# The first MLP's blocks 1 to 3 by seven products of quarters, and four modulations computed inside the retention heads

## The chip, the cores and the metric

The kernel runs on one core of a Trainium2 chip. The metric is device time in microseconds for one execution. A profile is taken of a separate execution; its own time stands beside its span.

## What is computed

One step of a two-layer network on 512 latent and 128 context tokens, 1024 channels each. Layer 0 mixes tokens by pooling, layer 1 by retention in four heads; each mixer is followed by an MLP of 4096 hidden channels with a squared ReLU. Before each sub-layer stands an RMS norm with a shift and a scale, behind it a gate; these six vectors of a layer (its modulations) come from the conditioning vectors by one linear map.

```python
def trunk(x, cond, ...):
    for i in range(DEPTH):
        mod = (silu(cond) @ w_ada[i] + b_ada[i])[:, None, :]
        sh_a, sc_a, g_a, sh_m, sc_m, g_m = split(mod, 6)
        h = rmsnorm(x, norm_mix_w[i]) * (1 + sc_a) + sh_a
        mix = pool_mixer(h) if i % 2 == 0 else retention_mixer(h)
        x = x + g_a * mix
        h = rmsnorm(x, norm_mlp_w[i]) * (1 + sc_m) + sh_m
        x = x + g_m * (square(relu(h @ mlp_w1[i])) @ mlp_w2[i])
    return rmsnorm(x, final_norm_w)
```

## The kernel before

**Layout.** The residual stream lies with channels on partitions: 8 tiles of 128 channels by 640 tokens (`xall`). Tokens are worked in two halves of 320. Every float32 product is made of three reduced-precision ones: both operands are split into a high and a low part (`split`, L142: ScalarE writes the high part, VectorE subtracts for the low one), and `mm3` (L202) issues high·high, high·low and low·high (L205, L206, L207). `gemm` (L209) runs them over the tiles of the inner dimension; an output tile of 128 channels over 1024 inner channels is 24 matmuls of 320 columns for each half.

**Weights.** `load` (L163) brings 1 MB of a weight matrix from HBM into one of two `wst` buffers by SyncE's DMA queue; `weights` (L183) splits it into two pairs `whi`, `wlo`. A third load waits until the splits of the first one are done.

**MLP.** `mlp` (L738) goes over four blocks of 1024 hidden channels. Each has a first product (`hidden`, L841, squares the ReLU and splits it) and a second one whose 8 output tiles are added to `xall` by `add_to_x` (L471, its instruction at L474). For the blocks named in `FAST` the first product is made by a scheme with seven products of quarters in place of eight: `quarters` (L756) forms sums of quarters of the activations once for the MLP, `seven` (L778) forms and splits seven sums of quarters of the weights for each half block (two loads of 1 MB, its first sum at L789), and `fast` (L800) runs the products and combines their results on VectorE. Before, only the second MLP (layer 1) does so, in blocks 1 to 3.

**Modulations.** `ada` (L272) is a generator; a call of `step` (L376) runs it by a piece. A modulation in mode "s s" is formed on VectorE: `sums` (L307) multiplies rows of 512 weights by one conditioning value and adds them up (L312, L314: 32 instructions of 512 columns), `turn_sums` (L316) turns the result by TensorE transposes (L320, 16 of them) and VectorE reduces (L321). `STEPS` says behind which output tile of the first MLP how many pieces run. Before, all six of layer 1 and the last one of layer 0 are made so inside the first MLP. Their weights land in `both` buffers of the MLP's own pool.

**Heads.** For each of the four retention heads: queries and keys (for heads 1 to 3 made at the end of the head before), state operands and decay tables on VectorE and ScalarE (`states`, L987; `attention`, L1023), the first two gate products (`gates`, L1010), the attention, two more gate products, the values of the next head (`values`, L964), the output product.

**Order.** The program is recorded in the order of the code, and a scheduler then places the instructions of each engine in one queue. An instruction waits on semaphores at its place in that queue.

Of the kernel before, what the change touches and what calls it, by code (L numbers as in the profile page):

```python
# [9 lines left out]
F32 = mybir.dt.float32  # L10
# [4 lines left out]
ALU = mybir.AluOpType  # L15
AX = mybir.AxisListType
PSUM = bass.MemoryType.PSUM

D = 1024
KD = D // 128  # L20
# [13 lines left out]
HALF = TOK // 2  # L34
# [16 lines left out]
MODE5 = "s s"  # L51
# [8 lines left out]
AHEAD = 1  # L60
FREE = 5

FAST = ((), (1, 2, 3))

STEPS = (((0, 0, 0, 0, 3, 2, 3, 0), (2, 1, 2, 1, 2, 1, 1, 1)),
# [3 lines left out]


def constants():
# [39 lines left out]
def hybrid_kernel(ctx: ExitStack, tc: tile.TileContext, x_prompt, x_sample, state_ret, c, c_ctx, w_ada, b_ada,  # L111
# [3 lines left out]
    V, S, G, T = nc.vector, nc.scalar, nc.gpsimd, nc.tensor  # L115
    uid = [0]

    def nm(s):
        uid[0] += 1
        return f"{s}_{uid[0]}"  # L120

    const = ctx.enter_context(tc.tile_pool(name="const", bufs=1))
# [4 lines left out]
    tmp = ctx.enter_context(tc.tile_pool(name="tmp", bufs=1))  # L127
# [3 lines left out]
    def bank():  # L131
        return psum.tile([128, 512], F32, tag="ps", name=nm("ps"))
# [30 lines left out]
    def load(src, shape, st=None):  # L163
        if not st:
            pool, n = extra[0] if extra else (wst, 2)
            if extra:
                extra.append(extra.pop(0))
            st = pool.tile([128, 2048], F32, tag="wst", name=nm("wst"), bufs=n)
        st = st.rearrange("p (a b) -> p a b", a=shape[0])
        nc.sync.dma_start(out=st, in_=src.rearrange("(k p) n -> p k n", p=128))  # L170
        return st
# [57 lines left out]
    ident = tab_sb[:, C_ID:C_ID + 128]  # L229
# [10 lines left out]
    c4 = const.tile([128, KD, 4], F32, name="c4")  # L240
# [7 lines left out]
    vec = const.tile([128, 168], F32, name="vec")  # L248
    O_MIX, O_MLP, O_PB, O_PS, O_FN, O_GN, O_B = 0, 16, 32, 40, 48, 56, 72
# [18 lines left out]
    ready = set()  # L268
# [3 lines left out]
    def ada(works, lag):  # L272
# [99 lines left out]
        if late:  # L372
            turn(*late.pop())

    def stepper(gen):
        def step(n=1, until=None):  # L376
            while n if until is None else until not in ready:
                try:
                    next(gen)
                except StopIteration:  # L380
                    return
                n -= 1
        return step
# [141 lines left out]
    with tc.tile_pool(name="pool", bufs=1) as pp:  # L525
# [9 lines left out]
        for word in FIRST.split():  # L535
            if word[0] == "a":
                astep(int(word[1:]))
            else:
                i = len(xt)
# [98 lines left out]
        run(PLAN[0])  # L638
        astep(until=(0, 2))

        ga = const.tile([128, KD, 2], F32, name="ga0")
        gb = const.tile([128, KD, 2], F32, name="gb0")
        V.tensor_tensor(ga, mod[0][2], vec[:, O_PS:O_PS + KD].unsqueeze(2).to_broadcast([128, KD, 2]), ALU.mult)
        V.tensor_tensor(gb, ga, vec[:, O_PB:O_PB + KD].unsqueeze(2).to_broadcast([128, KD, 2]), ALU.mult)
        V.tensor_scalar(ga, ga, -1.0, None, ALU.mult)
# [92 lines left out]
    def mlp(i, sq, norm, hm, step, along):  # L738

        with tc.tile_pool(name=f"hid{i}", bufs=1) as hid:  # L740
# [8 lines left out]
            def get(b, n):  # L749

                for o in range(1, AHEAD + 1):
                    if b * 8 + n + o < 64 and not ((b * 8 + n + o) // 16 in FAST[i] and (b * 8 + n + o) // 8 % 2 == 0):
                        gets[(b * 8 + n + o) // 8]((n + o) % 8)
                return gets[b](n)
# [45 lines left out]
            def fast(b, half, ops, take):  # L800

                col = b * 1024 + half * 512
                ws = seven(mlp_w1[i, :, col:col + 512])

                banks = {}
                w, u, v = next(ws), {}, {}
                for p, name in enumerate(("p1", "p5", "p6", "p7", "p5", "p1", "p7")):
                    after = next(ws, None)
                    for t in range(2):
                        fresh = (name, t) not in banks  # L810
                        if fresh:
                            banks[name, t] = bank()[:, 0:HALF]
                        ps = banks[name, t]
                        for k in range(4):
                            mm3(ps, [z[:, k, t * 128:t * 128 + 128] for z in w], ops[p][k], fresh and k == 0, k == 3, not fresh)
                        n = half * 4 + t
                        if p == 0:
                            u[t] = th()
                            S.copy(u[t], ps)
                        elif p == 2:  # L820
                            V.tensor_tensor(u[t], u[t], ps, ALU.add)
                        elif p == 3:
                            v[t] = th()
                            V.tensor_tensor(v[t], ps, u[t], ALU.subtract)
                            V.tensor_tensor(v[t], v[t], banks["p5", t], ALU.subtract)
                            take(n + 2, 1, v[t])
                        elif p == 4:
                            f = th()
                            V.tensor_tensor(f, u[t], ps, ALU.add)
                            take(n, 1, f)  # L830
                        elif p == 5:
                            take(n, 0, ps)
                        elif p == 6:
                            V.tensor_tensor(u[t], ps, u[t], ALU.subtract)
                            take(n + 2, 0, u[t])
                    w = after

            for b in range(4):
                act = [[hid.tile([128, TOK], F32R, tag=f"a{n}{e}", name=nm("a")) for e in "hl"] for n in range(8)]

                def hidden(n, h, ps):  # L841
                    r, f = th(), th()
                    S.activation(r, ps, AF.Relu)  # L843
                    S.activation(f, r, AF.Square)  # L844
                    split(f, *[z[:, HALVES[h]] for z in act[n]])

                def pair(n):
                    def take(h, out):
                        for j, ps in enumerate(out):
                            hidden(n + j, h, ps)  # L850
                    return [lambda j=j: get(0, n + j) for j in range(2)], hm, take

                if b == 0:
                    follow(sq, norm, [pair(0), pair(2)])
                if b in FAST[i]:
                    if b == FAST[i][0]:
                        ops = quarters()
                    for half in range(2):
                        fast(b, half, ops, hidden)
                    get(2 * b + 1, 0)  # L860
                else:
                    for n in range(4 if b == 0 else 0, 8):
                        if n == FREE:
                            room[0] = room[1]
                        for h in range(2):
                            hidden(n, h, gemm([get(2 * b, n)], hm, h)[0])
                        step(STEPS[b][0][n])
                        if i == 0 and b == 3 and n % 2:
                            next(logs, None)
                if i == 0 and b == 0:  # L870
                    step(until=(0, 5))
                if b == 3:
                    room[:] = [None, None]
                    return tail(lambda n, h: gemm([get(7, n)], act, h)[0], mod[i][5], along)
                for n in range(KD):
                    for h in range(2):
                        add_to_x(n, h, gemm([get(2 * b + 1, n)], act, h)[0], mod[i][5])
                    step(STEPS[b][1][n])

    step0 = stepper(ada([(i, m, MODE5 if i == 0 else "s s") for i, m in ((0, 5), (1, 1), (1, 0), (1, 2), (1, 4), (1, 3), (1, 5))], 0))  # L880
    h1 = []

    def norm1(h, d, r):
        if not h1:
            step0(until=(1, 5))
            h1.extend([scale_of(1, 1, O_MIX + KD), mod[1][0], [h_tiles(d) for d in range(KD)]])
        return norm_tile(h, d, r, *h1)

# [4 lines left out]
    with tc.tile_pool(name="ret", bufs=1) as rp:  # L893
# [231 lines left out]
        def norm2(h, d, r):  # L1125
            if not h2:
                h2.extend([scale_of(1, 4, O_MLP + KD), mod[1][3], [h_tiles(d) for d in range(KD)]])
            return norm_tile(h, d, r, *h2)

        for hd in range(HEADS):  # L1130
            gate = gates(hd)
            final = states(hd, qk[1], vv[1])
            next(final)
            attn = attention(hd, *qk, vv[0], vv[2])
            sg = [gate(e, between=final) for e in range(2)]
            us = gated(hd, gate, sg, *attn())
            get = weights(ret_w_out[0, hd * DV:(hd + 1) * DV])
            if hd < HEADS - 1:
                vv = values(hd + 1)
                for n in range(KD):  # L1140
                    for h in range(2):
                        add_to_x(n, h, gemm([get(n)], us, h)[0], mod[1][2])
                qk, _, singles = queries_keys(hd + 1)
                for u in singles:
                    u()
            else:
                sq = tail(lambda n, h: gemm([get(n)], us, h)[0], mod[1][2], normed(norm2))
# [74 lines left out]
```

## Time and profile before

| | us |
|---|---|
| median of 3 runs | 1649.18 (1647.44 to 1650.36) |
| the profiled execution, its own time | 1648.55 |
| its span, first to last instruction | 1646.4 |
| TensorE busy in the span | 1597.5 |
| VectorE busy | 1090.2 |
| ScalarE busy | 690.8 |

The span is what the profile covers; 2.15 us of the profiled execution's time lie around it. Busy time of TensorE counts matmuls that overlap in its pipeline, so it is presence of work rather than a rate; the rate is read from the number of matmuls in a stretch.

### The profile page before, as it was taken

Reading aid. Unit: us, or ns where it says so; the run is one execution under the profiler, and the core shown is the slowest. Engines: PE = TensorE matmul, PEld = TensorE weight load, DVE = VectorE, ACT = ScalarE, POOL = GpSimd, SP = SyncE. Lnnn points to the kernel's source line nnn. Section 1 sums busy time; section 2 is a strip of 40 time slices with the busy share of each in tenths; the row PEclk is TensorE's granted clock in tenths of the full one; section 3 lists DMA queues with packets and bytes.
Section 4 is the critical chain, followed back from the end, with each engine's and each line's share of the span. In section 5 each row is a group of like instructions: output and inputs, shape, how many; then the busy total and the mean of one; then the engine's idle time right before and its main releaser. Section 6 shows DMA issues by size and latency. Waiting matters only on the chain.

```text
span 1646.4 us, 24565 instructions
## 1 busy us (share of the span) xinstructions
PE 1597.5 (97%) x10041; PEld 1502.1 (91%) x10041; DVE 1090.2 (66%) x1958; ACT 690.8 (42%) x1258; POOL 74.1 (5%) x59
## 2 busy tenths in 40 slices
PE   7779999999999999999999999999989999999998
PEld 4348999999999998889988988998989999999998
DVE  6969996585585386665666557565976674564654
ACT  6665514314316345532633344253464262361540
POOL 3630000000000000000000000000200000000000
PEclk9989999999999999999999999999999999999999
DMA  9732655344332212202312230221112033131221
GB/s 350 249 128 103 207 181 176 128 154 154 129 113 93 77 52 77 103 32 73 114 39 74 81 103 26 77 97 58 52 54 98 30 103 103 52 103 52 94 74 65
DMA packets 125665, 169.83 MB, mean 103 GB/s; under 512 B 3512, under 2 KB 86896, under 8 KB 125552
## 3 DMA queue, kind: packets, MB, share of 16 engines
q1 hardware_dynamic: 122512, 161.28, 29.6%
q0 software_dynamic: 1312, 4.20, 0.7%
q10 hardware_dynamic: 1728, 2.78, 0.6%
q8 instruction: 79, 1.29, 0.3%
q14 instruction: 34, 0.28, 0.1%
HBM read 161.43 MB, written 6.82 MB: 102 GB/s over the span
## 4 chain that ended last, share of the span: by engine, by line
PE 92%; DVE 4%; ACT 1%; DMA 1%; issue 1%; POOL 0%; SPq 0%; ACTq 0%; DVEq 0%
PE ps L205 27%; PE ps L206 27%; PE ps L207 27%; PE ps L978 2%; PE ps L977 2%; PE ps L976 2%; PE ps L283 2%; PE ps L320 1%; DVE wlo L145 1%; DMA wst<-in_w_ada_dram 1%; ACT whi L144 1%; DVE df L622 0%; PE ps L439 0%; PE ps L604 0%; DVE t L145 0%
## 5 line engine op out<-in xcount | busy, mean ns | idle before, releaser
L144 ACT CAST whi<-wst 128x1024 fp32r<-128x1024 f32 x233 | 243.2, 1049 | 508.5 <-PE ps L206 438.4
L145 DVE TENSOR_TENSOR wlo<-wst,whi 128x1024 fp32r<-128x1024 f32 x220 | 269.6, 1230 | 157.1 <-ACT whi L144 156.4
L205 PE MATMUL ps<-a,whi 128*128 128x320 f32 x896 | 277.5, 310 | 0.0
L206 PE MATMUL ps<-a,whi 128*128 128x320 f32 x896 | 277.0, 309 | 0.0
L207 PE MATMUL ps<-a,wlo 128*128 128x320 f32 x896 | 276.9, 309 | 0.0
L474 DVE SCALAR_TENSOR_TENSOR xall<-ps,mod,xall 128x320 f32<-128x320 f32 (+2 forms) x288 | 117.2, 435 | 175.4 <-PE ps L207 174.1
L206 PEld LDWEIGHTS ps<-a,whi 128*128 128x128 f32 x896 | 168.2, 188 | 0.0
L205 PEld LDWEIGHTS ps<-a,whi 128*128 128x128 f32 x896 | 168.2, 188 | 0.0
L207 PEld LDWEIGHTS ps<-a,wlo 128*128 128x128 f32 x896 | 168.2, 188 | 0.0
L314 DVE SCALAR_TENSOR_TENSOR both<-both,c,both 128x512 f32<-128x512 f32 x182 | 126.0, 743 | 0.0
L145 DVE TENSOR_TENSOR a<-t,a 128x320 fp32r<-128x320 f32 x128 | 62.1, 487 | 48.1 <-ACT a L144 46.4
L207 PE MATMUL ps<-A,wlo 128*128 128x320 f32 x256 | 78.9, 309 | 0.0
L206 PE MATMUL ps<-A,whi 128*128 128x320 f32 x256 | 78.8, 309 | 0.0
L205 PE MATMUL ps<-A,whi 128*128 128x320 f32 x256 | 78.8, 310 | 0.0
L205 PE MATMUL ps<-h0h,whi 128*128 128x320 f32 x172 | 54.8, 325 | 9.7 <-ACT whi L144 6.4
L844 ACT ACTIVATE t<-t 128x320 f32<-128x320 f32 x128 | 60.5, 473 | 2.2
L144 ACT CAST a<-t 128x320 fp32r<-128x320 f32 x128 | 58.7, 459 | 2.4
L409 ACT ACTIVATE t<-xall 128x320 f32<-128x320 f32 x56 | 25.9, 469 | 80.3 <-DVE xall L474 80.1
L205 PE MATMUL ps<-h4h,whi 128*128 128x320 f32 x172 | 55.3, 324 | 3.5 <-ACT h4h L463 2.2
L843 ACT ACTIVATE t<-ps 128x320 f32<-128x320 f32 x92 | 39.7, 431 | 44.4 <-PE ps L207 44.4
L206 PE MATMUL ps<-h4l,whi 128*128 128x320 f32 x172 | 54.0, 314 | 1.4 <-DVE h4l L467 1.4
L206 PE MATMUL ps<-h3l,whi 128*128 128x320 f32 x172 | 53.5, 311 | 1.6 <-DVE h3l L467 1.6
(449 smaller groups left out, 4190.0 us busy)
## 6 DMA issues: line engine op xcount, KB each, us to landing
wst<-in_mlp_w_dram SPq DMA_DIRECT2D x64, 1024.0 KB, 5.1
both<-in_w_ada_dram SPq DMA_DIRECT2D x26, 1024.0 KB, 5.2
wst<-in_ret_w_in_dram SPq DMA_DIRECT2D x24, 1024.0 KB, 5.2
wst<-in_w_ada_dram SPq DMA_DIRECT2D x22, 1024.0 KB, 7.3
wst<-in_ret_w_out_dram SPq DMA_DIRECT2D x8, 1024.0 KB, 5.3
t<-in_state_ret_dram SPq DMA_DIRECT2D x16, 256.0 KB, 5.1
out_dram<-t POOLq DMA_DIRECT2D x16, 256.0 KB, 2.6
xt<-in_x_sample_dram SPq DMA_DIRECT2D x4, 512.0 KB, 4.1
```

Source lines behind the costliest of these rows:

```text
L144: S.copy(hi, src)
L145: sub.tensor_tensor(lo, src, hi.bitcast(F32), ALU.subtract)
L205: T.matmul(out, wh, ah, start=first, stop=False, skip_group_check=more)
L206: T.matmul(out, wh, al, start=False, stop=False, skip_group_check=more)
L207: T.matmul(out, wl, ah, start=False, stop=last, skip_group_check=more)
L283: T.matmul(pa, lhs[:, kk + k, :], z[:, k, :], start=first and k == 0 and j == 0, stop=last and k == 1 and j == len(w) - 1)
L314: V.scalar_tensor_tensor(acc[:, j], w[:, k], by, acc[:, j], ALU.mult, ALU.add)
L474: V.scalar_tensor_tensor(x, ps[:, cols], gate[:, d, j:j + 1], x, ALU.mult, ALU.add)
L843: S.activation(r, ps, AF.Relu)
L844: S.activation(f, r, AF.Square)
L976: T.matmul(out[i], hh[0], w[0][:, k, :], start=first, stop=False)
L977: T.matmul(out[i], hh[1], w[0][:, k, :], start=False, stop=False)
```

## The change

The first MLP's blocks 1 to 3 get the seven-product scheme too. Of the seven modulations that were made in the first MLP, one stays there as it was (layer 0's last, in block 0), two (layer 1's scale and shift of the mixer) are made in the second products of blocks 0 to 2 by a new generator, `ada_sums`, and four are made by the same generator in the heads, one at the start of each. `ada_sums` works a modulation in four quarters of 256 columns: one load of 1 MB into a `wst` buffer, 16 instructions on VectorE (2 without and 14 with an addend), 4 transposes, one reduction. Its two accumulators in the heads have one buffer each. In a head nothing of the program's own stands between the quarters. Since the generator stops only behind a quarter's sums, the call in a head ends with the first quarter of the next modulation.

```diff
-FAST = ((), (1, 2, 3))
-
-STEPS = (((0, 0, 0, 0, 3, 2, 3, 0), (2, 1, 2, 1, 2, 1, 1, 1)),
-         ((1, 1, 1, 1, 1, 0, 0, 0), (2, 1, 2, 1, 2, 1, 1, 1)),
-         ((1, 1, 1, 1, 1, 0, 0, 0), (2, 1, 2, 1, 2, 1, 1, 1)),
-         ((1, 1, 1, 1, 1, 0, 0, 0), ()))
+FAST = ((1, 2, 3), (1, 2, 3))
+
+STEPS = (((0, 0, 0, 0, 3, 2, 3, 0), (0, 0, 0, 0, 1, 0, 1, 0)),
+         ((), (0, 1, 0, 1, 0, 1, 0, 0)),
+         ((), (0, 1, 0, 1, 0, 1, 0, 0)),
+         ((), ()))
...
+    def ada_sums(works, place):
+        for i, m in works:
+            for q in range(4):
+                col = m * D + q * 256
+                w = load(w_ada[i, :, col:col + 256], (8, 256))
+                acc = place()
+                for k in range(KD):
+                    for j in range(2):
+                        by = c4[:, k, j:j + 1]
+                        if k == 0:
+                            V.tensor_scalar(acc[j], w[:, k], by, None, ALU.mult)
+                        else:
+                            V.scalar_tensor_tensor(acc[j], w[:, k], by, acc[j], ALU.mult, ALU.add)
+                yield
+                pt = bank()
+                for j in range(2):
+                    for k in range(2):
+                        T.transpose(pt[:, (2 * j + k) * 128:(2 * j + k + 1) * 128], acc[j][:, k * 128:(k + 1) * 128], ident)
+                V.tensor_reduce(mod[i][m][:, q * 2:q * 2 + 2, :], pt.rearrange("p (j n k) -> p n j k", j=2, n=2),
+                                axis=AX.X, op=ALU.add)
...
+    def modulations():
+        yield from ada([(0, 5, MODE5)], 0)
+        yield from ada_sums([(1, 1), (1, 0)], lambda: [tmp.tile([128, HALF], F32, tag="sqacc", name=nm("acc"),
+                                                                bufs=2)[:, 0:256] for _ in range(2)])
...
+        step1 = stepper(ada_sums([(1, 2), (1, 4), (1, 3), (1, 5)], lambda: [rp.tile(
+            [128, 256], F32, tag=f"acc{j}", name=nm("acc")) for j in range(2)]))
         for hd in range(HEADS):
             gate = gates(hd)
             final = states(hd, qk[1], vv[1])
             next(final)
             attn = attention(hd, *qk, vv[0], vv[2])
+            step1(until=(1, (2, 4, 3, 5)[hd]))
             sg = [gate(e, between=final) for e in range(2)]
```

In the changed file the lines behind `ada_sums` stand some 26 to 32 further down: the transposes of the new generator are L394, its sums L387 and L389, its reduction L395.

**TensorE at the start of head 1, before.** The rows go from the last matmuls of the head's keys (`ps_7868`) to its first gate product (`ps_7947`); L991 transposes the context's keys (`pr`).

```order
L206 MATMUL ps_7868<-h7l_5776,whi_7830 128x320
L207 MATMUL ps_7868<-h7h_5775,wlo_7831 128x320
L991 MATMUL ps_7903<-tab_sb,pr_7607 128x128
L205 MATMUL ps_7947<-h0h_5761,whi_7943 128x320
L206 MATMUL ps_7947<-h0l_5762,whi_7943 128x320
L207 MATMUL ps_7947<-h0h_5761,wlo_7944 128x320
```

**The same place in the change.** The keys end with `ps_7945`, the gate product is `ps_8129`; `acc` are the accumulators of the modulation, two to a quarter.

```order
L207 MATMUL ps_7945<-h7h_5727,wlo_7908 128x320
L1023 MATMUL ps_7980<-tab_sb,pr_7684 128x128
L394 MATMUL ps_8017<-tab_sb,acc_6653 128x128 x2
L394 MATMUL ps_8017<-tab_sb,acc_6654 128x128 x2
L1023 MATMUL ps_7980<-tab_sb,pr_7687 128x128
L394 MATMUL ps_8043<-tab_sb,acc_8025 128x128 x2
L394 MATMUL ps_8043<-tab_sb,acc_8026 128x128 x2
L394 MATMUL ps_8069<-tab_sb,acc_8051 128x128 x2
L394 MATMUL ps_8069<-tab_sb,acc_8052 128x128 x2
L394 MATMUL ps_8095<-tab_sb,acc_8077 128x128 x2
L394 MATMUL ps_8095<-tab_sb,acc_8078 128x128 x2
L205 MATMUL ps_8129<-h0h_5713,whi_8125 128x320
```

The 16 transposes of a modulation, four quarters, stand between the keys and the first gate product. In heads 1 to 3 the first quarter's accumulators (here `acc_6653`, `acc_6654`) were summed in the head before; head 0 has all four quarters there.

**SyncE's queue at the same place, in the change.** `wst` are the two weight buffers in turn; `wst_7688` and `wst_7832` are the head's query and key weights, `wst_8123` its first gate weights.

```order
L170 DMA wst_7688<-in_ret_w_in_dram 128x8x256
L170 DMA wst_7832<-in_ret_w_in_dram 128x8x256
L170 DMA wst_8023<-in_w_ada_dram 128x8x256
L170 DMA wst_8049<-in_w_ada_dram 128x8x256
L1073 DMA t_8002<-in_state_ret_dram 128x512
L170 DMA wst_8075<-in_w_ada_dram 128x8x256
L170 DMA wst_8102<-in_w_ada_dram 128x8x256
L170 DMA wst_8123<-in_ret_w_in_dram 128x8x256
```

Before, the gate weights followed directly on the key weights; now four loads for modulations stand between them (three in head 3, which has no next modulation). VectorE's queue has the 16 sums of the quarters `acc_8051`, `acc_8077` and of the next head's `acc_8104` one behind the other, and `wlo_8126`, the low part of the first gate weights, one place ahead of the last sum of `acc_8105`.

## Rows read from the trace of the kernel before

**Rows 1.** The page: busy time of TensorE and loader; the ended-last chain by engine.
```profile
PE 1597.5 (97%) x10041; PEld 1502.1 (91%) x10041; DVE 1090.2 (66%) x1958; ACT 690.8 (42%) x1258; POOL 74.1 (5%) x59
...
PE 92%; DVE 4%; ACT 1%; DMA 1%; issue 1%; POOL 0%; SPq 0%; ACTq 0%; DVEq 0%
```
**Rows 2.** Waits of TensorE in 600 to 1180, the longest: us, times, longest.
```profile
PE ps L978 <- DVE wlo L145: 1.0, 1, 1.0
```
**Rows 3.** Busy us and instructions by stretch, then clock, DMA: first MLP, second MLP.
```profile
350.00:450.00 100.00, 100.00 (x690) 99.98 (x689) 67.07 (x108) 35.77 (x62) 0.00 (x0) 1.00 0.45 147
...
1400.00:1500.00 100.00, 100.00 (x682) 99.74 (x681) 57.56 (x86) 41.28 (x73) 0.00 (x0) 1.00 0.24 78
```
**Rows 4.** The chain that ended last, in order: a modulation's eight transposes, two blocks apart.
```profile
234.72 0.87 PE ps L320 x8
...
466.94 0.87 PE ps L320 x8
```
**Rows 5.** First sum of `seven` in the second MLP: ns, first and last start.
```profile
L789 DVE TENSOR_TENSOR wst<-wst x2: 1225/1226/1228, 1291.4 to 1329.6; 128x1024 f32<-128x1024 f32 x2
...
L789 DVE TENSOR_TENSOR wst<-wst x6: 1215/1225/1228, 1291.4 to 1542.4; 128x1024 f32<-128x1024 f32 x6
```
**Rows 6.** VectorE's timeline in the first MLP: start, us, line, instruction, count.
```profile
220.41 1.28 DVE L321 TENSOR_REDUCE mod<-ps 128x4 f32<-128x512 f32 x2
221.60 0.87 DVE L312 TENSOR_SCALAR both<-both,c 128x512 f32<-128x512 f32 x2
...
231.24 0.55 DVE L474 SCALAR_TENSOR_TENSOR xall<-ps,mod,xall 128x320 f32<-128x320 f32 x1
231.71 3.39 DVE L314 SCALAR_TENSOR_TENSOR both<-both,c,both 128x512 f32<-128x512 f32 x5
235.02 0.67 DVE L474 SCALAR_TENSOR_TENSOR xall<-ps,mod,xall 128x192 f32<-128x192 f32 x2
```
**Rows 7.** Groups by line and form: busy us, mean ns of one, idle before.
```profile
L145 DVE TENSOR_TENSOR wlo<-wst,whi 128x1024 fp32r<-128x1024 f32 x220 | 269.6, 1230 | 157.1 <-ACT whi L144 156.4
L144 ACT CAST whi<-wst 128x1024 fp32r<-128x1024 f32 x233 | 243.2, 1049 | 508.5 <-PE ps L206 438.4 <-PE ps L977 50.1 <-PE ps L283 7.2
...
L145 DVE TENSOR_TENSOR r<-t,r 128x512 fp32r<-128x512 f32 x32 | 22.0, 688 | 14.5 <-ACT r L144 13.8
```
**Rows 8.** Line L998, VectorE instructions of 256 columns: ns least, median, most.
```profile
L998 DVE SCALAR_TENSOR_TENSOR t<-ps,zeta,t x8: 475/481/484, 664.1 to 1102.4; 128x256 fp32r<-128x256 f32 x8
```
**Rows 9.** One of the page's DMA issues: KB each, median us to landing.
```profile
wst<-in_mlp_w_dram SPq DMA_DIRECT2D x64, 1024.0 KB, 5.1
```
**Rows 10.** TensorE's timeline at the start of head 1: last key matmul, first gate matmul.
```profile
806.25 0.31 PE L207 MATMUL ps<-h7h,wlo 128*128 128x320 f32 x1
...
806.42 0.39 PE L205 MATMUL ps<-h0h,whi 128*128 128x320 f32 x1
```
**Rows 11.** VectorE's timeline there, from the last key's rotation to the state operand.
```profile
808.67 0.35 DVE L932 TENSOR_TENSOR t<-ps,tab_sb 128x192 f32<-128x192 f32 x1
...
812.56 0.62 DVE L1035 TENSOR_TENSOR dm<-dm,t 128x448 f32<-128x448 f32 x1
814.65 0.69 DVE L953 TENSOR_REDUCE cm<-t 128x1 f32<-128x512 f32 x1 [1.47 <-DMA t<-in_state_ret_dram]
```
**Rows 12.** Start of head 0: VectorE's centring and tables, and TensorE's last value matmul.
```profile
656.28 1.37 DVE L953 TENSOR_REDUCE cm<-ps 128x1 f32<-128x512 f32 x2
...
667.83 0.68 DVE L1044 TENSOR_TENSOR t<-q,xi 128x512 f32<-128x512 f32 x1
...
660.61 0.39 PE L978 MATMUL ps<-wlo,h7h 128*128 128x512 f32 x1
```
**Rows 13.** Stretches after TensorE's wait at the first MLP's start; clock third from last.
```profile
138.50:140.00 1.50, 1.06 (x4) 1.06 (x5) 1.50 (x4) 1.31 (x3) 0.00 (x0) 0.54 1.04 403
140.00:142.00 2.00, 2.00 (x9) 2.00 (x8) 2.00 (x6) 1.00 (x2) 0.00 (x0) 0.50 1.05 394
142.00:144.00 2.00, 2.00 (x15) 2.00 (x15) 2.00 (x5) 1.25 (x3) 0.00 (x0) 0.99 1.04 385
```

More of the change, by code (lines that the diff above doesn't have):

```diff
@@ L373, in ada @@
             turn(*late.pop())
+    def ada_sums(works, place):
[18 more added lines that the diff above has]
+                                axis=AX.X, op=ALU.add)
+            ob = O_B + i * 48 + m * KD
+            V.tensor_tensor(mod[i][m], mod[i][m], vec[:, ob:ob + KD].unsqueeze(2).to_broadcast([128, KD, 2]), ALU.add)
+            ready.add((i, m))
     def stepper(gen):
@@ L639, in hybrid_kernel @@
         astep(until=(0, 2))
-        ga = const.tile([128, KD, 2], F32, name="ga0")
-        gb = const.tile([128, KD, 2], F32, name="gb0")
+        ga = pp.tile([128, KD, 2], F32, name="ga0")
+        gb = pp.tile([128, KD, 2], F32, name="gb0")
         V.tensor_tensor(ga, mod[0][2], vec[:, O_PS:O_PS + KD].unsqueeze(2).to_broadcast([128, KD, 2]), ALU.mult)
@@ L859, in mlp @@
                         fast(b, half, ops, hidden)
+                        if i == 0 and b == 3:
+                            next(logs, None)
+                            next(logs, None)
                     get(2 * b + 1, 0)
@@ L867, in mlp @@
                         step(STEPS[b][0][n])
-                        if i == 0 and b == 3 and n % 2:
-                            next(logs, None)
                 if i == 0 and b == 0:
@@ L878, in mlp @@
                     step(STEPS[b][1][n])
-    step0 = stepper(ada([(i, m, MODE5 if i == 0 else "s s") for i, m in ((0, 5), (1, 1), (1, 0), (1, 2), (1, 4), (1, 3), (1, 5))], 0))
+    def modulations():
+        yield from ada([(0, 5, MODE5)], 0)
+        yield from ada_sums([(1, 1), (1, 0)], lambda: [tmp.tile([128, HALF], F32, tag="sqacc", name=nm("acc"),
+                                                                bufs=2)[:, 0:256] for _ in range(2)])
+    step0 = stepper(modulations())
     h1 = []
@@ L884, in norm1 @@
         if not h1:
-            step0(until=(1, 5))
+            step0(until=(1, 0))
             h1.extend([scale_of(1, 1, O_MIX + KD), mod[1][0], [h_tiles(d) for d in range(KD)]])
```

## The prediction

> **What bounds the kernel now.** I read the page first. TensorE is busy for 97% of the span and the chain that ended last is TensorE for 92% of it [rows 1]: time is saved by taking matmuls away, and lost wherever TensorE's queue stands still. Then its waits: over the retention heads the longest is 1.0 us [rows 2]. Then its rate: 690 matmuls of 320 columns in 100 us of the first MLP, 0.145 us each [rows 3]. At the start of head 1 the last key matmul begins at 806.25 and the first gate matmul at 806.42, one step later [rows 10]; VectorE's work for the head, from 808.67 on [rows 11], lies beside the gate product. So a head's start now costs TensorE nothing, and that is the place to watch. VectorE is busy for 66% of the span [rows 1], but a share says nothing about a queue in which TensorE's next instruction waits for VectorE's last.
>
> The sum is made against the profiled execution, 1648.55 us; the median of the runs is 0.6 higher.
>
> **First MLP, seven products.** A block's first product falls from 384 to 336 matmuls, 48 × 0.145 = 7.0 us, 20.9 us for three blocks. Blocks as they run give another figure. In the first MLP two transpose groups exactly two blocks apart stand at 234.72 and 466.94 [rows 4], 116.1 us a block, of which four groups of 0.87 us are transposes: 112.6. In the second MLP, where blocks already run by seven products, L789 of the second half of block 1 stands at 1329.6 and that of block 3 at 1542.4 [rows 5]: 106.4 a block. I take the measured difference, 6.2 × 3 = **-18.6**; the ends are -20.9 by count and, with 106.4 against 768 bare matmuls (111.3), -14.7. The added sums of weights and results on VectorE and ScalarE are those of the second MLP, where VectorE is busy for 58% [rows 3]; they lie beside the matmuls, and if that cover went, rows 3's 682 matmuls in 100 us would fall.
>
> **Transposes.** Eight take 0.87 us [rows 4], 0.109 each. The four moved modulations take 64 with them: **-7.0** here; they come back inside the heads' stretches below.
>
> **The two modulations that stay** cost eight quarters of VectorE's time in second products. A quarter's price: five sums of 512 columns take 3.39 us, so (3.39 - 0.74) / 4 = 0.66 from start to start; 512 columns fewer make a subtraction cheaper by 1230 - 688 = 542 ns [rows 7], so 256 fewer by 0.27, which leaves 0.39. Upper end 0.48, an instruction of 256 columns standing alone [rows 8]; lower end 0.33, half of 0.66. The two without addend: 0.87 for a pair of 512 columns [rows 6], 0.26 each at half width. The reduction: 0.6 of rows 6's pair. Together 14 × 0.39 + 0.52 + 0.6 = 6.6 us. [...] An output tile lasts 48 × 0.145 = 7.0 us, with 2.5 us of its own on VectorE (0.55 + 0.67 [rows 6], 1.23 [rows 7]). A quarter does not fit beside that in one tile, but only every second tile has one, so I cost it at nothing, with one exception. In block 0 the last quarter's sums stand behind tile 6's add: they end some 8.3 us after tile 7 began (1.2 + 0.6 + 6.5), only then is the buffer free for the second weight load of block 1, 5.1 us [rows 9], then two sums, a cast and a low part, 1.2 + 1.2 + 1.2 (the cast beside the second sum). That is 17 us, and TensorE wants it after 7.0 + 24 × 0.145 = 10.5. **+6**; ends 0 and, if blocks 2 and 3 had the same, 18. There the last quarter comes one tile earlier, which just covers it.
>
> **The heads.** Here each quarter's transposes wait for its sums, the next quarter's sums wait for those transposes (one buffer for each accumulator), and TensorE's queue has the gate product behind all of them. Nothing in the queue covers it. From quarter to quarter: 6.6 and 0.4 for the hand-over, 7.0 us. Head 1, from the end of the last key matmul, t = 0: VectorE's rotation and tables take 813.18 - 808.67 = 4.5 us [rows 11], starting at some 0.9 (two copies by ScalarE come first), a reduction and the two first sums 1.1, to 6.5; 14 sums 5.5 and, between them, the state operand 2.2 (0.69 [rows 11], a scaling, and two more of 512 columns at 0.69 [rows 7]), to 14.2. Two more quarters: 28.2. The buffer of the first gate weights is that of the last of these quarters: load 5.1 [rows 9] and cast 1.05 [rows 7], to 34.4. VectorE goes on with the next head's first quarter, to 35.2, and the weights' low part is beside its end: TensorE runs freely at 36.0. Less 1.0 of matmuls that go on in between: 35.0. Head 2 the same. Head 3 has no next modulation, so its gate weights get a buffer one quarter earlier: 28. Head 0 has four quarters: the first runs from 656.3, beside the last value matmuls (the last begins at 660.61 [rows 12]), and ends 1.5 behind them; centring takes 7.8 (656.28 to L998's first start at 664.1 [rows 12, 8]) and the tables 3.2 (from there to 668.51 [rows 12], less a low part of weights), reduction and first sums 1.1, to 13.6; then as above + 29.5, 43.1; less 1.0: 42. Sum 42 + 35 + 35 + 28 = **+140**, transposes included. With 213 sums on this path the ends are -13 (0.33 each) and +19 (0.48); if the gate weights came no later than the quarters, -22.
>
> **Clock.** After TensorE's wait at the first MLP's start the granted clock is 0.54 and 0.50 to 142 and 0.99 in the next 2 us [rows 13], the lower and the upper of its two levels (1.2 and 2.4 GHz); with 1.06 us of matmuls before 140 that is 3 us at half speed, 1.5 lost. Four heads: **+6**; ends 0 and 10.
>
> **Sum:** 1648.55 - 18.6 - 7.0 + 6 + 140 + 6 = **1775** us.
>
> **Rivals.**
> 1. *Heads hidden, faster.* The sums end before TensorE needs the gate product, because VectorE has room (66%). For it: the sums need only weights and conditioning values, and VectorE idles during the key products. Against it: accumulators with one buffer and transposes that stand behind the key matmuls, so quarters two to four cannot begin there. It decides if TensorE could go on to the gate product past waiting transposes. Then only the seven products count: 1648.55 - 18.6 = 1630. The Trainium skill, page "TensorE: Matmul & The Clock Gate", section "Step-by-step: what each phase is for", says that matmuls stay in program order and only weight loads are drawn ahead; rows 2 have no place that tests it.
> 2. *Gate weights in time.* The stretches end with the third new quarter, as in head 3: 1775 - 22 = 1753. Against it: SyncE's queue has four loads ahead, in two buffers.
> 3. *First MLP starved.* The eight loads in `wst` take every second place, and each makes a following weight late by its landing time, 8 × 5.1 = 41 us in place of the 6: 1810. For it: before, these loads had buffers of their own. Against it: the weights' splits are recorded a tile ahead.
>
> That the change does not do what it says is no rival: 48 matmuls a block are gone from the program.
>
> **Numbers.** Forecast 0.72, rival 2 0.14, rival 3 0.08, rival 1 0.06. The bounds of the single terms, not all at one end, give 1745 to 1805; rival 3 takes the upper end to 1812, and rival 1 is left out. A difference of 0.2%, 3.3 us, is about what a measurement of this kernel can tell from none. Faster 0.05 (rival 1), within it 0.01, slower 0.94.
>
> **What would show it.** Four waits of TensorE for VectorE's accumulators, before L394, of 5 to 20 us each in every head, and one for ScalarE's `whi` and VectorE's `wlo` at the first gate product of heads 0 to 2 but not 3; sums of 256 columns 0.39 us apart; blocks 2 and 3 of the first MLP near 106 us plus 1.3 of transposes; L789's counterpart waiting for its load at block 1. I am wrong if TensorE's chain in the heads shows no VectorE, or if the first MLP is not shorter by some 20 us.

## The result, and the profile after

The change makes the kernel slower: 1770.93 us (median of 4 runs, 1769.45 to 1773.01) against 1648.75 (4 runs). The ratio is 1.0741, 95% interval 1.0723 to 1.076. The profiled execution took 1771.07 us, its span is 1769.3.

From the page after: busy time, the ended-last chain by engine, and two groups (busy us, mean ns of one, idle time ahead and what ended it).

```profile
PE 1600.1 (90%) x9897; PEld 1490.0 (84%) x9897; DVE 1208.5 (68%) x2300; ACT 702.7 (40%) x1296; POOL 73.2 (4%) x59
...
PE 76%; DVE 13%; DMA 6%; ACT 3%; issue 1%; POOL 0%; ACTq 0%; DVEq 0%
...
L389 DVE SCALAR_TENSOR_TENSOR acc<-wst,c,acc 128x256 f32<-128x256 f32 x336 | 137.9, 478 | 0.6
L394 PE MATMUL ps<-tab_sb,acc 128*128 128x128 f32 x96 | 22.3, 354 | 95.6 <-DVE acc L389 95.6
```

Beside [rows 1]: TensorE falls from 97% to 90% of a longer span at nearly the same busy time (1597.5 and 1600.1 us, with 144 matmuls fewer), and VectorE rises from 4% to 13% of the chain. VectorE works 118 us more, but its share hardly rises, from 66% to 68%: the share does not show that it now works at moments when TensorE waits for it.

TensorE's waits over the heads (total us, times, longest), the answer to [rows 2]:

```profile
PE ps L394 <- DVE acc L389: 95.6, 19, 13.8
PE ps L205 <- ACT whi L144: 16.5, 3, 5.6
```

112 us of waits stand where the longest was 1.0. TensorE's timeline at the start of head 0 shows how they lie (start, us; in brackets the wait ahead and who ended it):

```profile
646.89 0.60 PE L394 MATMUL ps<-tab_sb,acc 128*128 128x128 f32 x4
661.26 1.09 PE L394 MATMUL ps<-tab_sb,acc 128*128 128x128 f32 x4 [13.77 <-DVE acc L389]
668.10 0.69 PE L394 MATMUL ps<-tab_sb,acc 128*128 128x128 f32 x2 [5.75 <-DVE acc L389]
...
675.10 0.69 PE L394 MATMUL ps<-tab_sb,acc 128*128 128x128 f32 x2 [5.40 <-DVE acc L389]
...
682.26 0.63 PE L205 MATMUL ps<-h0h,whi 128*128 128x320 f32 x1 [5.56 <-ACT whi L144]
```

Four groups of transposes, a quarter of a modulation each, and behind them the first gate product. The first group does not wait: its sums lay beside the values' product (VectorE's lines stand further down, with the forecast for head 0). The second waits through VectorE's centring, tables and sums, the others for one quarter each, the gate product for its weights. The chain that ended last names the links of the final stretch: sums, the landing of the gate weights, their cast, the gate product.

```profile
670.69 4.76 DVE acc L389 x12
675.51 0.37 issue
675.99 5.16 DMA wst<-in_ret_w_in_dram
681.16 1.05 ACT whi L144
682.26 0.63 PE ps L205
```

VectorE in head 1 gives the price of a quarter:

```profile
845.46 5.35 DVE L389 SCALAR_TENSOR_TENSOR acc<-wst,c,acc 128x256 f32<-128x256 f32 x13
850.74 0.35 DVE L387 TENSOR_SCALAR acc<-wst,c 128x256 f32<-128x256 f32 x1
...
857.74 0.35 DVE L387 TENSOR_SCALAR acc<-wst,c 128x256 f32<-128x256 f32 x1
```

857.74 - 850.74 = 7.0 us a quarter, and (5.35 - 0.48) / 12 = 0.41 us from sum to sum.

Where the 122.9 us of the span went, by the first transpose of the context's keys in each head (660.8, 806.4, 952.4, 1098.4 before; 646.7, 829.7, 1011.2, 1192.4 after):

| stretch | before | after | difference | predicted |
|---|---|---|---|---|
| up to TensorE's wait at the first MLP's start | 135.2 | 136.7 | +1.5 | 0 |
| first MLP, queries, keys and values of head 0 | 525.6 | 510.0 | -15.6 | -19.6 |
| head 0 | 145.6 | 183.0 | +37.4 | +43.5 |
| head 1 | 146.0 | 181.5 | +35.5 | +36.5 |
| head 2 | 146.0 | 181.2 | +35.2 | +36.5 |
| head 3 and the rest | 548.0 | 576.9 | +28.9 | +29.5 |

The prediction stands with the clock's 1.5 us put into each head. The first row is no part of the change: in the thirteen kernels of this study, whose programs hardly differ up to there, it lay between 133.9 and 140.2.

### The profile page after: what moved, and what is told of

It is laid out like the page before. It is cut to its first block, busy times and chain, and to the rows that moved or that the text cites. A ratio compares the mean times of both kernels' runs of the same rounds, so it can differ in the third digit from the quotient of the medians.

```text
span 1769.3 us, 24646 instructions
## 1 busy us (share of the span) xinstructions
PE 1600.1 (90%) x9897; PEld 1490.0 (84%) x9897; DVE 1208.5 (68%) x2300; ACT 702.7 (40%) x1296; POOL 73.2 (4%) x59
## 4 chain that ended last, share of the span: by engine, by line
PE 76%; DVE 13%; DMA 6%; ACT 3%; issue 1%; POOL 0%; ACTq 0%; DVEq 0%
PE ps L205 22%; PE ps L206 22%; PE ps L207 22%; DVE acc L389 4%; DMA wst<-in_mlp_w_dram 4%; PE ps L1010 2%; PE ps L1009 2%; PE ps L1008 2%; DVE wlo L145 2%; ACT whi L144 2%; PE ps L283 1%; DMA wst<-in_ret_w_in_dram 1%; DMA wst<-in_w_ada_dram 1%; PE ps L394 1%; DVE mod L395 1%
## 5 line engine op out<-in xcount | busy, mean ns | idle before, releaser
L144 ACT CAST whi<-wst 128x1024 fp32r<-128x1024 f32 x251 | 260.6, 1048 | 534.7 <-PE ps L206 282.3
L145 DVE TENSOR_TENSOR wlo<-wst,whi 128x1024 fp32r<-128x1024 f32 x238 | 290.7, 1229 | 156.1 <-ACT whi L144 155.4
L205 PEld LDWEIGHTS ps<-a,whi 128*128 128x128 f32 x896 | 168.0, 188 | 0.8 <-ACT a L144 0.8
L389 DVE SCALAR_TENSOR_TENSOR acc<-wst,c,acc 128x256 f32<-128x256 f32 x336 | 137.9, 478 | 0.6
L394 PE MATMUL ps<-tab_sb,acc 128*128 128x128 f32 x96 | 22.3, 354 | 95.6 <-DVE acc L389 95.6
L394 PEld LDWEIGHTS ps<-tab_sb,acc 128*128 128x128 f32 x96 | 13.2, 172 | 102.4 <-issue 86.1
L207 PE MATMUL ps<-tq,wlo 128*128 128x320 f32 x288 | 89.0, 309 | 0.0
L205 PE MATMUL ps<-tq,whi 128*128 128x320 f32 x288 | 89.0, 309 | 0.0
L206 PE MATMUL ps<-tq,whi 128*128 128x320 f32 x288 | 89.0, 309 | 0.0
L205 PE MATMUL ps<-h0h,whi 128*128 128x320 f32 x148 | 48.0, 332 | 30.9 <-ACT whi L144 27.6
```

Source lines behind the costliest of these rows:

```text
L144: S.copy(hi, src)
L145: sub.tensor_tensor(lo, src, hi.bitcast(F32), ALU.subtract)
L205: T.matmul(out, wh, ah, start=first, stop=False, skip_group_check=more)
L206: T.matmul(out, wh, al, start=False, stop=False, skip_group_check=more)
L207: T.matmul(out, wl, ah, start=False, stop=last, skip_group_check=more)
L389: V.scalar_tensor_tensor(acc[j], w[:, k], by, acc[j], ALU.mult, ALU.add)
```

## Experiments

Three theories were tried. **A**, the prediction's: TensorE stands in program order at the transposes until VectorE has made the sums that lie one behind the other. **B**: the modulations' loads of 1 MB through two weight buffers set the pace. **C** differs by run, as its expectation says; mostly: VectorE has no room for the sums, so they cost time wherever they stand.

**1. The first MLP's change alone** (label mlp_alone).

```diff
+    for m in range(2, 6):
+        G.memset(mod[1][m], 0.0)
...
-            step1(until=(1, (2, 4, 3, 5)[hd]))
```

> Four of layer 1's modulations are left out (their vectors are zero); the first MLP is that of the change. Theory A (TensorE stands, in program order, at the modulations' transposes until VectorE has made the sums): nothing stands at the head starts any more, the heads' period is again 145.8 to 146.0 us, and only the first MLP's change is left. In the traces of before and of the change TensorE's first transpose behind head 0's values stands at 660.6 and 646.9, so 13.7 less: 1648.6 - 13.7 = 1635 us. Theory B (the added loads of 1 MB set the spacing of the quarters): the same here. Theory C (the seven products in the first MLP themselves cost time that shows later, in the heads): the head starts keep part of their waits, 1650 us or more.

Measured: 1634.32 us, ratio 0.9909 (0.9895 to 0.9924). TensorE's longest wait in 600 to 1180:

```profile
PE ps L1012 <- DVE wlo L145: 1.0, 1, 1.0
```

The heads' periods are 145.8, 146.0 and 146.0 again. So the four modulations at the heads' starts cost 1770.9 - 1634.3 = 136.6 us, more than the change's whole loss of 122, and the seven products leave nothing behind there.

**2. The heads' change alone** (label heads_alone): the first MLP's blocks 1 to 3 by eight products, the decay tables where the kernel before has them.

```diff
-FAST = ((1, 2, 3), (1, 2, 3))
+FAST = ((), (1, 2, 3))
...
+                        if i == 0 and b == 3 and n % 2:
+                            next(logs, None)
```

> The change without its seven products: the first MLP's blocks 1 to 3 run eight products, the modulations are made where the change makes them. Theory A: the heads cost what they cost in the change (183.0, 181.4, 181.2 us a period), and the first MLP gets its 6.2 us a block back: 1771 + 18.6 = 1790 us. The wait of 4.8 us at block 1 may go as well, since an eight-product block needs one load there where the seven-product one needs two: 1785 to 1790. Theory C: the heads' periods become shorter than 181 us, below 1780.

Measured: 1782.23 us, ratio 1.081 (1.0794 to 1.0827). Neither expectation holds: the heads' periods (183.5, 182.2, 182.7) rule out C, and the total lies under A's 1785. Measured from the first MLP's opening wait to the eighth output tile of its last second product (first half of the tokens), this kernel needs 433.2 us, the change 424.3, so the seven products bring 8.9 there and not 18.6. Block by block (from the first output tile of one second product to that of the next) it is 112.9, 114.0 and 114.0 here against 115.5, 107.7 and 109.8: block 2 gains 6.3 as predicted, block 1 loses 2.6, block 3 gains 4.2. Of the total, some 2.2 is the start of the program (138.9 against 136.7). What blocks 1 and 3 lose is found in runs 6 and 8.

**3. A second pair of accumulators in the heads** (label two_acc).

```diff
+        turns = []
+
+        def place():
+            turns.append(0)
+            if len(turns) % 2:
+                return [rp.tile([128, 256], F32, tag=f"acc{j}", name=nm("acc")) for j in range(2)]
+            return [tmp.tile([128, HALF], F32, tag="sqacc", name=nm("acd"), bufs=2)[:, 0:256] for j in range(2)]
-        step1 = stepper(ada_sums([(1, 2), (1, 4), (1, 3), (1, 5)], lambda: [rp.tile(
-            [128, 256], F32, tag=f"acc{j}", name=nm("acc")) for j in range(2)]))
+        step1 = stepper(ada_sums([(1, 2), (1, 4), (1, 3), (1, 5)], place))
```

> The accumulators of the modulations in the heads get a second pair of buffers, in turn with the first; the work and the place of the call are the same. In VectorE's queue one more quarter's sums then stand ahead of the head's start, beside the products before it. Theory A: one quarter of 7.0 us less on the path in each of four heads, 28 us: 1743 us, TensorE's waits for accumulators in a head 16 to 18 us where they were 23.5. Theory B (loads set the spacing): the second quarter's load must still wait for a buffer, no more than 2 us a head, 1763 us or more. Theory C: no difference.

Measured: 1744.82 us, ratio 1.0586 (1.0568 to 1.0603), 26.1 less than the change; A said 28. TensorE's waits over the heads (`acd` is the second pair):

```profile
PE ps L394 <- DVE acc L389: 50.4, 4, 13.8
PE ps L394 <- DVE acd L389: 22.4, 4, 5.6
PE ps L205 <- ACT whi L144: 16.2, 3, 5.5
```

72.8 us in place of 95.6, 5.7 a head: with two pairs the scheduler puts one more quarter's sums ahead of the head's start, where they lie beside matmuls. C falls; B would have let the loads keep the pace, and falls too.

**4. Half the sums, all the loads** (label half_sums).

```diff
-    def ada_sums(works, place):
+    def ada_sums(works, place, rows=KD):
...
-                for k in range(KD):
+                for k in range(rows):
...
-            [128, 256], F32, tag=f"acc{j}", name=nm("acc")) for j in range(2)]))
+            [128, 256], F32, tag=f"acc{j}", name=nm("acc")) for j in range(2)], 4))
```

> The modulations of the heads are summed over half of their 1024 rows (8 sums a quarter in place of 16); the loads stay as they are, 1 MB each. Theory A: 8 x 0.406 = 3.2 us less for each quarter that is on the path. These are 3 in head 0 and 4 (the next head's first included, since the gate weights' low part stands behind it), 4 and 3 in the others, 14 in all: 45 us less, 1726 us, unless the loads, at 5.1 us to landing, then set the spacing: 7.0 - 5.1 = 1.9 for each, 27 less, 1744 us. Theory B: no difference, 1765 to 1771 us.

Measured, once only: 1732.47 us, 38.5 less, between A's two values and below the 1744 at which the loads would have set the pace. The waits over the heads:

```profile
PE ps L394 <- DVE acc L389: 58.0, 17, 9.3
PE ps L205 <- ACT whi L144: 17.6, 4, 5.5
```

The wait for accumulators falls by 37.6, the wait for the gate weights stays. The heads' periods fall from 183.0, 181.5 and 181.2 to 173.2, 172.9 and 171.7, by 8.6 to 9.8 each. That is three quarters a head at 3.2 and not the expected four in heads 1 and 2: the next head's first quarter, which shares the last stretch, is not on the path there; the load of the gate weights is. B falls with this run: 48 sums of 0.41 us a modulation set the pace, not its loads.

**5. Gate weights ahead of the quarters** (label gates_ahead).

```diff
-            gate = gates(hd)
             final = states(hd, qk[1], vv[1])
             next(final)
             attn = attention(hd, *qk, vv[0], vv[2])
+            gate = gates(hd)
...
             get = weights(ret_w_in[0, :, 4096 + hd * DV:4096 + (hd + 1) * DV])
+            get(0), get(1)
```

> The change, with each head's first gate weights loaded and split ahead of the modulation's quarters instead of behind them. Theory A: in heads 0 to 2 the gate product then begins right behind the last transposes, and the waits for the weights' high part (16.5 us in all in the change) go: 1771 - 16.5 = 1754 us; the four waits for accumulators stay. Theory B (the queue of loads sets the spacing): the gate weights now stand ahead of the quarters' loads in the same two buffers and make each second quarter late by their 5.1 us, so nothing is won: 1766 us or more.

Measured: 1753.95 us, ratio 1.0644 (1.0625 to 1.0663), 17.0 less, as A said. The wait for the high part is gone and the accumulators' is what it was:

```profile
PE ps L394 <- DVE acc L389: 95.0, 16, 13.8
PE ps L206 <- DVE h4l L493: 2.6, 1, 2.6
```

It also tests TensorE's order. In head 1 of this kernel the low part of the gate weights is made long ahead,

```profile
810.95 1.23 DVE L145 TENSOR_TENSOR wlo<-wst,whi 128x1024 fp32r<-128x1024 f32 x1 [1.16 <-ACT whi L144]
```

and no later weights are cast before 858; the gate product had its weights (whether the place for its result was free the trace does not show), and TensorE stood before the transposes ahead of it in its queue:

```profile
837.21 1.09 PE L394 MATMUL ps<-tab_sb,acc 128*128 128x128 f32 x4 [11.80 <-DVE acc L389]
844.15 0.66 PE L394 MATMUL ps<-tab_sb,acc 128*128 128x128 f32 x2 [5.85 <-DVE acc L389]
```

**6. The boundary of blocks 0 and 1** (label boundary). In the change TensorE waits there once; the wait, the chain that leads to it, and the stretches behind it (granted clock third from last):

```profile
PE ps L205 <- ACT whi L144: 4.8, 1, 4.8
```

```profile
254.82 3.18 DVE acc L389 x8
258.02 5.36 DMA wst<-in_mlp_w_dram
263.47 1.24 DVE wst L815
264.73 1.05 ACT whi L144
265.82 0.64 PE ps L205
```

```profile
264.00:266.00 2.00, 0.18 (x1) 0.18 (x2) 1.97 (x3) 1.06 (x2) 0.00 (x0) 0.50 0.00 0
...
268.00:270.00 2.00, 2.00 (x10) 2.00 (x9) 1.97 (x3) 0.49 (x1) 0.00 (x0) 0.50 0.00 0
270.00:272.00 2.00, 2.00 (x14) 2.00 (x14) 1.96 (x3) 1.79 (x3) 0.00 (x0) 0.87 0.00 0
```

The last sums of block 0's quarter free the buffer at 258.0, the weights land 5.4 later, L815 (L789 of the kernel before) adds them, ScalarE casts. TensorE then runs at the lower of its two levels for some 4 us more.

```diff
-STEPS = (((0, 0, 0, 0, 3, 2, 3, 0), (0, 0, 0, 0, 1, 0, 1, 0)),
+STEPS = (((0, 0, 0, 0, 3, 2, 3, 0), (0, 0, 0, 1, 0, 1, 0, 0)),
```

> The change, with block 0's last two quarters one output tile earlier each (behind tiles 3 and 5 in place of 4 and 6), as blocks 1 and 2 have them. If the wait of 4.8 us at the start of block 1 comes from the last quarter's sums holding the weight buffer, it goes, and with it the matmuls at half clock that follow it (some 17 of them 0.27 us apart in place of 0.145, 2.1 us): 1771 - 7 = 1764 us. If the second weight load is late for another reason (VectorE's other work in that tile), the wait stays: 1770 us.

Measured: 1763.73 us, ratio 1.0697 (1.0683 to 1.0712), 7.2 less, as expected. In block 1 the one wait of TensorE left is

```profile
PE ps L205 <- DVE t L851: 1.1, 1, 1.1
```

and the block takes 109.3 in place of 115.5.

**7. The quarters spread over the heads** (labels spread and spread_boundary). The call at the head's start goes; single calls stand behind pieces of the heads' matmuls.

```diff
-            step1(until=(1, (2, 4, 3, 5)[hd]))
...
+                sg.append(gate(e, between=final))
+                step1(hd == 0)
             us = gated(hd, gate, sg, *attn())
+            step1(hd < 2)
...
                 vv = values(hd + 1)
+                if hd == 0:
+                    step1(until=(1, 2))
...
+                    step1(n in ((3, 6), (1, 5), (1, 5))[hd])
...
+                    step1(j == 1)
...
             for e in range(2):
+                if e and hd:
+                    step1()
                 st = load(ret_w_in[0, e * 512:(e + 1) * 512, c0:c0 + 512], (4, 512))
```

> The same modulations by the same sums in the heads, with one call at a time behind pieces of the heads' matmuls: in head 0 behind each of the first two gate products, behind the gating and before the output product, then behind two output tiles and the second of the four query and key products; in heads 1 and 2 inside the values' product, and so on. Theory A: the transposes come a stage after the sums and nobody waits. What is left against the run without the four modulations (1634 us) is 64 transposes, 7.0 us: 1641 us, up to 1650 if a weight load or two come late. Theory C (VectorE has no room: 16 quarters of 7.0 us displace its other work): up to 112 us more than 1634, 1690 us or more.

Measured: 1670.59 us, ratio 1.0136 (1.012 to 1.0152). 100 us of the loss are gone, yet the time lies 20 above the upper end that A gave, and C's 1690 isn't reached. The waits over the heads tell of the rest:

```profile
PE ps L207 <- DVE wlo L145: 4.8, 2, 3.0
PE ps L1010 <- ACT whi L144: 4.0, 2, 2.1
PE ps L1012 <- DVE wlo L145: 3.8, 3, 2.4
PE ps L394 <- DVE acc L389: 2.8, 2, 2.0
```

The first three are late weights: of the values' products, of head 0's output product and of head 1's queries and keys. The periods are 168.0, 156.7 and 148.2: head 0, which asks for eight quarters (three of their sums lie within 36 us around the values' product, since the call ahead of the output product ends one modulation and begins the next), loses 22 us, head 1 with five 11, head 2 with three 2.

> The two edits before it together. Theory A: 1641 - 7 = 1634 us, 0.9% faster than the kernel before. Theory C: as in the run before it, 1690 us or more.

Measured: 1664.33 us, ratio 1.0094 (1.0078 to 1.011): 6.3 less than the run before it, so the boundary's gain adds up; A's 1634 is missed by the same late weights.

**8. Better places** (labels spread2 and spread3). The first modulation has a generator of its own, so that its end doesn't begin the next; nobody asks for a quarter behind the gating or right ahead of the output product; the decay tables' three parts stand in block 2's second half and block 3's two halves.

```diff
+        step1 = stepper(ada_sums([(1, 2)], place))
+        step2 = stepper(ada_sums([(1, 4), (1, 3), (1, 5)], place))
...
+                (step2 if hd else step1)(hd in (0, 3) or e == 0)
...
+                    step2(n in (1, 5))
...
+                if e:
+                    (step2 if hd > 1 else step1)()
...
-                        if i == 0 and b == 3:
-                            next(logs, None)
+                        if i == 0 and 2 * b + half > 4:
                             next(logs, None)
```

> The spread version again, with no quarter at the places where the run before showed TensorE waiting for weights (behind the gating and right ahead of the output product): the first modulation gets a quarter in the values' product of head 0, one behind each of the head's two gate products, one in the next values' product; the other three get one behind the first gate product, one in the values' product and two in the output product of a head. Block 0's quarters stand as in the boundary run, and the decay tables' three parts are spread over blocks 2 and 3 of the first MLP. Theory A: at these places the sums lie beside matmuls and the loads beside free buffers, so 1634 - 7 (boundary) - 2 (decay tables) + 7 (transposes) = 1632 us, and up to 1645 if two or three weight loads in the values' product still come late. Theory C (VectorE has no room): about the time of the run before, 1664 us, since the same number of sums is made.

Measured: 1644.41 us, ratio 0.9974 (0.9965 to 0.9983), 20 less than the run before it with as many sums: C falls. Block 3 of the first MLP takes 107.2 where it took 109.8, so its missing 2 us had been the decay tables, which the change put into one place. Head 0 still costs 9 us: the scheduler had moved the transposes of head 0's keys in front of the values' product, and TensorE waited for them.

spread3 asks for that first quarter at the start of head 0's gates instead (`step1(hd == 0)` ahead of them, and `if e and hd` in the values).

> The run before it, with the first quarter of the first modulation asked for at the start of head 0's gates instead of inside the values' product of head 0, where the scheduler had pulled the transposes of head 0's keys in front of the values and TensorE waited 3.5 us for them, with some 1.5 us at half clock behind. Theory A: 1644 - 5 = 1639 us. If the 9 us that head 0 costs come from its six quarters as such (theory C), no difference: 1644 us.

Measured: 1640.85 us, ratio 0.9939 (0.9925 to 0.9952), 3.6 less: this version is faster than both kernels, than the kernel before by 0.6%. TensorE's longest wait in 600 to 1180 is

```profile
PE ps L207 <- DVE wlo L145: 2.0, 1, 2.0
```

Heads 1 and 2 of it (busy us of TensorE, its loader, VectorE, ScalarE and GpSimd, then the clock):

```profile
791.70:939.40 147.70, 147.44 (x865) 135.56 (x863) 113.52 (x243) 57.01 (x103) 2.16 (x4) 1.00 0.30 100
939.40:1087.10 147.70, 147.45 (x864) 135.54 (x863) 112.28 (x241) 56.05 (x102) 2.16 (x4) 1.00 0.30 100
```

and head 1 of the kernel before:

```profile
806.40:952.40 146.00, 145.76 (x848) 133.87 (x846) 88.07 (x173) 57.42 (x103) 2.15 (x4) 1.00 0.22 73
```

VectorE does 25 us more in a head, and the head is longer by 1.7, the price of its 16 transposes (16 x 0.109 [rows 4]).

**9. What the seven products are worth there** (label spread3_eight): spread3 with the first MLP's `FAST` empty.

> The run beside it with the first MLP's blocks 1 to 3 by eight products again. With no wait at block 1 and the decay tables spread in both, the difference of the two is the seven products alone: by the traces 6.2 us a block, 18.6 us, 1658 us, slower than the kernel before by the transposes and late loads in the heads. If the seven products are worth only what the run of the heads alone suggested (11.3 us), 1650 us.

Measured: 1655.03 us, ratio 1.0025 (1.0013 to 1.0036), 14.2 more than spread3, between the two expectations. In the first MLP itself, between the same two points as in run 2, it is 433.2 against 415.1: 18.1 us, the prediction's 18.6. Against that, from the first output tile of head 3's output product to the end spread3 needs 484.0 us and this one 478.1, with the same code; TensorE shows 3.3 us of waits for VectorE's `t` (L851) in the second MLP of spread3 and none here. Why is left open.

## Why the prediction was right

Forecast 1775, measured 1771. The mechanism was the one predicted, and it is shown: without the four modulations the loss is gone (run 1), with half the sums each head is shorter by half of three quarters' sums (run 4), with the sums spread TensorE hardly stands, 2.0 us at most (run 8). Step by step:

- **Quarter price, 7.0 us; 0.39 us a sum** (from rows of 512 columns [rows 6 to 8]): 7.0 and 0.41. At 0.41 the 64 narrow sums of a modulation take 26 us of VectorE's time, where 32 of 512 columns at 0.66 took 21.
- **Seven products, -18.6**: 18.1 by run 9, where neither the boundary's wait nor the decay tables stand in the way.
- **Four waits for accumulators in each head, a wait for the gate weights in heads 0 to 2 and not in 3**: the waits for the weights are as said, for `whi` alone. For accumulators there are three waits of 5 to 14 us in each head, not four: in every head the first of the four groups finds its sums done. For heads 1 to 3 the sum itself went by three; only the list of signs said four. Of head 3 the trace has no row for `whi`, only

```profile
PE ps L394 <- DVE acc L389: 23.3, 4, 11.8
PE ps L1023 <- ACT pr L956: 0.5, 1, 0.5
```

  (one of these 4 waits is 0.16 us). Heads 1, 2 and 3 are within 1.3 us of the forecast.
- **Head 0, +42: 6 too much.** The failed step is "the first runs from 656.3, beside the last value matmuls", and the 13.6 us up to the second quarter's first sums that were built on it. VectorE had been idle beside the values, the first quarter was done before they ended, and the second quarter's first sum stands at 647.31 among the centring:

```profile
627.45 5.63 DVE L389 SCALAR_TENSOR_TENSOR acc<-wst,c,acc 128x256 f32<-128x256 f32 x14
641.42 0.69 DVE L985 TENSOR_REDUCE cm<-ps 128x1 f32<-128x512 f32 x1 [8.34 <-PE ps L1010]
...
647.31 0.35 DVE L387 TENSOR_SCALAR acc<-wst,c 128x256 f32<-128x256 f32 x1 [0.30 <-PE ps L394]
```

  The transposes of the second quarter come 14.4 us behind the first ones, where the sum had 21.3; the clock (below) takes 0.8 of these 6.9 us back.
- **Blocks 2 and 3 near 106 plus 1.3**: block 2 takes 107.7 as said, block 3 109.8. The calls for the decay tables, which the change moves, were given no price; run 8 shows 2.6 us.
- **Boundary, +6**: the wait is 4.8 for the reason given, L815 waiting for its load; the term left out the 2.3 us lost at the lower clock behind it. Run 6 measures both, 7.2. Rival 3's eight such places did not come: the other seven quarters delay no weights.
- **Clock, 1.5 a head**: too low for head 0, near for the others. Behind the last wait of head 0, then of head 1:

```profile
682.00:684.00 2.00, 1.74 (x5) 1.32 (x6) 2.00 (x5) 1.98 (x3) 0.00 (x0) 0.50 0.00 0
684.00:686.00 2.00, 2.00 (x9) 2.00 (x8) 1.19 (x2) 0.46 (x1) 0.00 (x0) 0.50 0.36 80
686.00:688.00 2.00, 2.00 (x12) 2.00 (x12) 0.00 (x0) 0.00 (x0) 0.00 (x0) 0.77 1.06 372
...
864.00:866.00 2.00, 2.00 (x5) 1.47 (x6) 2.00 (x4) 1.98 (x2) 0.00 (x0) 0.50 0.00 0
866.00:868.00 2.00, 2.00 (x9) 2.00 (x9) 1.13 (x2) 0.20 (x1) 0.00 (x0) 0.54 0.43 105
```

  In head 0 the matmuls run from 682.26 to 686 at the lower level (0.50 of 2.4 GHz is 1.2) and two us at 0.77, which loses 2.3 us. By the same reading it is 1.9 in head 1, 1.6 in head 2 and 1.4 in head 3: 7.2 together in place of 6.
- **Errors that cancelled, which was luck**: the sum had the first MLP 4.0 us too short (clock at the boundary, decay tables) and left out 1.5 of the program's start; it had head 0 6.1 too long and the other heads 2.9. The forecast lies 3.9 above the profiled execution. The sign "shorter by some 20 us" for the first MLP was missed: its stretch is shorter by 15.6.
- **Rival 2** (gate weights in time) had -22; run 5 puts that edit at -17.0. **Rival 1** was wrong for this placing of the call, and nearly right for another one (1641 in spread3 against its 1630): by runs 7 to 9 the sums can be hidden, but not behind transposes that stand ahead of the next matmul in TensorE's queue. That order is what the Trainium skill, page "TensorE: Matmul & The Clock Gate", section "Step-by-step: what each phase is for", states: matmuls stay in program order. Run 5 agrees: with the gate weights ready, 11.8 us of waiting for accumulators still stood ahead of the gate product.

## What to carry to other kernels

An engine with idle time does not hide work by having it; the work must be recorded a stage ahead of the instruction that needs it, on both queues. Ask of each inserted wait what stands behind it on its own engine: here 16 small transposes, 1.7 us of work, held up TensorE for 28 us a head. Where a piece can be placed freely, put its consumer a stage after its producer, and look which weight buffer its load takes from whom.

## What had not been expected of the hardware

A wait of some 5 us costs TensorE more than its length, since matmuls run at half rate behind it: at the boundary the granted clock is 0.50 until 270 and 0.87 in the 2 us behind, after head 0's last wait 0.50 until 686 and 0.77 until 688, some 2.3 us lost at each place, more than the 1.5 that the prediction took from the first MLP's start. The boundary's wait of 4.8 us, for which the prediction counted no clock at all, cost 7.2 (run 6).
